# A decoder trunk's attention stage: the second half's query projections in two-tile passes spread over the units, rows turned eight steps behind their tile, norm sums issued later

## The chip, the cores and the metric

The kernel runs on one core of one Trainium2 chip. The metric is the time of one execution on the device in microseconds (us); lower is better. Before the change three runs gave a median of 1218.23 us, from 1217.66 to 1218.72. The engines of a core are TensorE (PE in the profile, with its weight loads as PEld), VectorE (DVE), ScalarE (ACT), GpSimd (POOL) and SyncE (SP). Each runs its own instructions in the order in which they were built and waits on semaphores for the others; DMA queues are fed by SP and POOL.

## The reference

512 tokens of width 1024, batch 1, float32 throughout. A recurrent layer comes first (norm, gated linear recurrence, output projection, feed-forward), then keys and values are made once from its result, then an attention layer (8 query heads of 128 in two groups that share a key/value head, three dilated windows) and a second feed-forward. The change lies in the attention layer, and one line of it in the first norm. Cut to that:

```
h = x + recurrent_mixer(rms_norm(x, a_norm), ...);  h = h + swiglu(rms_norm(h, a_ffn_norm), ...)
k, v = shared_kv(h, ...)                            # per dilation group g = 0, 1, 2: k normed, rotated
q = (rms_norm(h, b_norm) @ b_w_q)                   # 512 x (3 groups x 8 heads x 128)
q = rope(rms_norm(q, b_q_norm[g]))                  # per head
for each group g, window / dilation (128/1, 512/4, 2048/16):
    s = q k^T / sqrt(128), masked to the band;  p = exp(s - max) / sum
    o_g, lse_g = p v, max + log(sum)
o = sum over g of softmax(lse)_g * o_g              # so: one softmax over the keys of all groups
h = h + o @ b_w_o;  h = h + swiglu(rms_norm(h, b_ffn_norm), ...)
```

## The kernel before, in words

**Numbers.** A float32 product is made of three fp32r matmuls. Each operand is split into a rounded high half (xh, wh, qh, kh, ph, vh) and the remainder as a low half (xl, wl, ql, kl, pl, vl), and high·high, low·high and high·low are summed in PSUM (L146 to L148; in the row projections L703 to L705). Splitting an activation is an ACT copy (L228) and a DVE subtraction (L229).

**Weights.** They come as a stream of 128x1024 pieces in order of use (class Stream). SP loads a piece into wr (L85; two buffers), ACT copies it to the high half wh (L100). For the pieces of the attention layer ACT then writes the negated piece to wl (L103), and POOL issues a DMA that reads the piece from memory once more and adds it to wl (L104). Three buffers of wh and wl; in the attention stage a piece is split two pieces ahead of its use.

**Row projections.** `project` takes four pieces, each with two of the eight 128-row blocks of the inner dimension and 512 output columns (four heads). For each piece it goes over the token tiles of 128 given to it; the six matmuls of one piece and tile are a *step*, behind which the generator yields. So a pass over four tiles is 16 steps, one over two tiles is 8 steps, and each reads its four pieces once. When a tile is complete, `collect` has DVE write the gained rows to kn (L637), ACT square them in place (L639) and DVE reduce the squares to sqc (L640). One step later the first 32 elements of each head are rotated (four DVE instructions, L649 to L652). One step after a pass's last tile the normalising factors are made (L661 and the eight small instructions of `rsqrt`, L210 to L219), then a tile's rows are scaled at each step (L669), and `lag` steps after the last tile, one tile a step, PE transposes them (L781) and ACT copies them out as qt (L783). A step is counted by `tick`; `at(steps, fn)` queues work for a later tick.

**Attention.** It runs over 32 units (half kv, query block n, phase p). Unit u's scores are multiplied at stage u (L146 to L148 on kh and qh; the first unit of a block also has the query halves made from qt, L228 and L229), followed by the softmax: masked minimum on DVE (L846 to L849), exponential on ACT (L854), reciprocal on DVE (L855), scaling on POOL (L856). Three units later PE transposes the probabilities pr (L868) and they are split into ph and pl; four units later, at every second unit, the values are multiplied. The first half (kv = 0) has its queries projected ahead of all this; the second half's projections and the first half of the output projection fill PE between the units.

**What sets the order.** The filling is a table written by hand. Each entry names a generator, how many steps of it are given, and over which stretch of units these are spread evenly:

```
drain(itertools.islice(q1, START_Q))          # START_Q = 11 steps ahead of the first unit
plan = [(q1, 40 - START_Q, 0, 12), (q1, 4, 12, 15), (q1, 4, 15, 18.5), (o0, 16, 20, 37)]
```

Here q1 is the second half's projections: groups 0 and 1 over all four tiles, group 2 first over tiles 0 and 1, then over 2 and 3, so its four pieces come twice. o0 is the first half of the output projection. The finished outputs of the first half are split into xh and xl (`move`) when the 4 steps of the second entry have been given, because they take the place of the projections' input. Since a tick is also counted at every second stage of the units, a lag in steps is shorter than that many projections.

The softmax and the split of the turned probabilities are built at high priority, so a scheduler may put them ahead of other work on DVE and ACT. In the first norm, too, the sums are built at high priority.

**The first norm.** The input projection starts on unnormalised rows, and the norm factors are made meanwhile. `in_block(2)` and `in_block(3)` call `between` behind one of their eight inner steps: in block 2 it issues the matmuls of the column sums of squares (L245), in block 3 those that spread the factors over rows.

Of the kernel before, what the change touches and what calls it, by code (L numbers as in the profile page):

```python
# [15 lines left out]
F32 = mybir.dt.float32  # L16
# [123 lines left out]
def trunk(tc, A, out):  # L140
# [11 lines left out]
    def add_pieces(aps, kind="", but=0):  # L152

        start = len(pieces)
        pieces.extend((a, "" if but and i % but == 0 else kind) for i, a in enumerate(aps))
        return start
# [11 lines left out]

    p_f1 = ffn_pieces("f1_in", "f1_out")
    p_kv = add_pieces([A["w_kv"][i] for i in range(12)])  # L170
    p_q = add_pieces([A["w_q"][i] for i in (*range(24), *range(20, 24))], "dma")
    p_o = add_pieces([A["w_o"][i] for i in range(8)], "dma")
    p_f2 = ffn_pieces("f2_in", "f2_out")

    with tc.tile_pool(name="keep", bufs=1) as kp, tc.tile_pool(name="wts", bufs=3) as wp, \
# [104 lines left out]
        with tc.tile_pool(name="lru", bufs=2) as lp, \  # L280
# [16 lines left out]
            def in_block(i, tag="mm", between=None):  # L297
                ps = bank(tag)
                wh, wl = ws.get(i)
                for k in range(KB):  # L300
                    c = slice(128 * k, 128 * k + 128)
                    mm3(ps, (wh[:, c], wl[:, c]), (xh[k], xl[k]), k == 0, k == KB - 1)
                    if k == 2 and between:
                        between()
                return ps

# [188 lines left out]
        with tc.tile_pool(name="tables", bufs=1) as rp:  # L495
# [14 lines left out]
            with tc.tile_pool(name="att", bufs=2) as ap:  # L510
                ap = Pool(ap)
# [12 lines left out]
STATS = 5  # L524
N_PR = 4
LAG_T, LAG_V = 3, 4
START_Q = 11


def rotary(tc, A, rp, tp):  # L530
# [67 lines left out]
def attention(tc, A, ap, ws, env):  # L598
# [30 lines left out]
    def collect(raw, nh, j, n, st, tab, g_row):  # L629

        if j == 0:
            st["sq"] = ap.tile([128, n * nh], F32, name="sqc", tag=f"sqc{nh}").rearrange("q (t i) -> q t i", i=nh)
            st["kn"] = []
        dst = ap.tile([128, 512], F32, name="kn", tag="kn", bufs=N_KN)
        rows = raw[:, :128 * nh]
        x = dst.rearrange("q (h d) -> q h d", d=128)[:, :nh]
        V.tensor_tensor(x, rows.rearrange("q (h d) -> q h d", d=128),  # L637
                        grow[:, g_row].unsqueeze(1).to_broadcast([128, nh, 128]), ALU.mult)
        S.activation(rows, rows, AF.Square)  # L639
        V.tensor_reduce(st["sq"][:, j], rows.rearrange("q (i d) -> q i d", i=nh), mybir.AxisListType.X, ALU.add)  # L640
        st["kn"].append(dst)
        at(1, lambda: rotate(x, nh, tab))
# [48 lines left out]
    def project(p0, xh, xl, done, tiles=range(4)):  # L691

        ps = [None] * 4
        for kk in range(4):
            wh, wl = ws.get(p0 + kk)
            for t in tiles:
                r = slice(128 * t, 128 * t + 128)
                if kk == 0:
                    ps[t] = bank(next(free))
                for k2 in range(2):  # L700
                    k = 2 * kk + k2
                    c = slice(512 * k2, 512 * k2 + 512)
                    PE.matmul(ps[t], xh[k][:, r], wh[:, c], start=k == 0, stop=False)  # L703
                    PE.matmul(ps[t], xh[k][:, r], wl[:, c], start=False, stop=False)  # L704
                    PE.matmul(ps[t], xl[k][:, r], wh[:, c], start=False, stop=k == 7)  # L705
                if kk == 3:
                    done(t, ps[t])
                tick()
                yield
# [59 lines left out]
    qt = {}  # L769

    def project_q(kv):
        for g in range(3):

            for j, tiles in enumerate((range(2), range(2, 4)) if kv and g == 2 else (range(4),)):
                def done_q(t, ps, g=g, st={}, tiles=tiles):
                    collect(ps, 4, t - tiles[0], len(tiles), st, t, 3 + g)
                    if t == tiles[-1]:
                        def turn(j, rows):
                            pt = bank("PT")
                            for i in range(4):  # L780
                                PE.transpose(pt[:, 128 * i:128 * i + 128], rows[:, 128 * i:128 * i + 128], ident)  # L781
                            q = ap.tile([128, 4, 4, 32], F32, name="qt", bufs=12)
                            S.copy(q, pt.rearrange("q (h p i) -> q p h i", h=4, p=4))  # L783
                            qt[j, kv, g] = q
                            if not kv and not j:
                                query_part(0, 0, g)

                        normed(st, 4, 0, turn, 8 if len(tiles) > 2 else 5, tiles)

                yield from project(p_q + 12 * kv + 4 * g + 4 * j, xh, xl, done_q, tiles)  # L790

    def first(fn):

# [9 lines left out]
    def query_part(kv, n, g):  # L803
        if kv and n % 2:
            tags = (f"kh{g}0", f"kl{g}0", 1)
        else:
            tags = ("qh", "ql", 3)
        qh, ql = [ap.tile([128, 512], F32R, name=x, tag=x, bufs=tags[2]) for x in tags[:2]]
        halve(qt.pop((n, kv, g)).rearrange("q p h i -> q (p h i)"), qh, ql)
        qs_[kv, n, g] = qh, ql  # L810
# [127 lines left out]
    drain(project_q(0))  # L938
    q1, o0 = project_q(1), out_half(0, lambda m: None)
    drain(itertools.islice(q1, START_Q))  # L940
    plan = [(q1, 40 - START_Q, 0, 12), (q1, 4, 12, 15), (q1, 4, 15, 18.5), (o0, 16, 20, 37)]
    given, stage = [0] * len(plan), {}
    for k, u in enumerate(attend()):
        stage[u] = stage.get(u, 0) + 1
# [92 lines left out]
```

## Time and profile before

| | |
|---|---|
| median of three runs | 1218.23 us (1217.66 to 1218.72) |
| the profiled execution's own time | 1220.25 us |
| its span | 1218.3 us |
| mean granted clock of PE | 0.998 |
| busy, share of the span: PE | 1204.8 us, 99% |
| DVE | 658.2 us, 54% |
| ACT | 514.4 us, 42% |
| POOL | 157.2 us, 13% |
| weight pieces of w_q, each loaded once and added once by DMA | 28 x 512 KB |

The profile is one execution taken by the hardware profiler. Its span runs from the first instruction to the last. Busy times of engines overlap and don't add up to the span. In a timeline row stand the start, the duration, the engine, the line of the kernel, the operation with its output and inputs, and in brackets the idle time in front of it on its engine and what ended that. In a group's row stand the number of instructions, their busy time with the mean of one in ns, and the idle time in front. Matmuls are pipelined, so that consecutive rows of PE overlap and the time of a block is best taken from the start of one row to the start of another. The attention stage with its projections lies at about 640 to 830 us of the span; its units fill about 690 to 825 us.

### The profile page before, as it was taken

How to read it: one execution, taken by the hardware profiler on the slowest of the kernel's cores; microseconds unless marked ns; L12 is line 12 of the kernel's file. 1: busy time of each engine (PE TensorE's matmuls, PEld its weight loads, DVE VectorE, ACT ScalarE, POOL GpSimd, SP SyncE). 2: the span in 40 equal slices, each digit the busy share in tenths (PEclk: the TensorE clock that was granted, in tenths of full speed). 3: DMA queues.
4: the chain of work that ended last, by engine and by line, in shares of the span. 5: the costliest groups of instructions: out<-in, count | busy, mean ns of one | idle time of the engine just before them, and what ended most of it. 6: DMA issues, size and time to landing. Idle time of an engine off the chain costs nothing.

```text
span 1218.3 us, 14685 instructions
## 1 busy us (share of the span) xinstructions
PE 1204.8 (99%) x5627; PEld 995.6 (82%) x5627; DVE 658.2 (54%) x1237; ACT 514.4 (42%) x758; POOL 157.2 (13%) x159
## 2 busy tenths in 40 slices
PE   8999999999999999999999999999999999999998
PEld 6778888888888888888888887898888888888887
DVE  7787674454544333377564567765554455542221
ACT  6795433233232222265555667655423232222110
POOL 0100001011110000010411243341011011110000
PEclk9999999999999999999999999999999999999999
DMA  6643333323233333333988666335223323233341
GB/s 237 145 104 104 104 106 104 104 87 103 87 103 100 89 100 96 100 96 94 227 179 178 135 153 151 79 70 137 88 87 104 103 88 104 87 100 112 113 115 44
DMA packets 40757, 137.62 MB, mean 113 GB/s; under 512 B 5104, under 2 KB 5744, under 8 KB 40688
## 3 DMA queue, kind: packets, MB, share of 16 engines
q1 hardware_dynamic: 32976, 112.00, 28.9%
q0 software_dynamic: 6704, 23.60, 11.0%
q10 hardware_dynamic: 1008, 1.09, 0.3%
q8 instruction: 44, 0.72, 0.2%
q14 instruction: 25, 0.20, 0.0%
HBM read 133.53 MB, written 2.10 MB: 111 GB/s over the span
## 4 chain that ended last, share of the span: by engine, by line
PE 94%; DVE 3%; ACT 2%; DMA 1%; issue 0%; SPq 0%; DVEq 0%; ACTq 0%
PE ps L147 25%; PE ps L148 25%; PE ps L146 25%; PE ps L703 5%; PE ps L705 5%; PE ps L704 5%; DMA wr<-in_w_in 1%; PE ps L781 1%; PE ps L868 1%; PE ps L387 1%; PE ps L386 1%; ACT wh L100 0%; DVE sqc L640 0%; PE ps L245 0%; DVE pl L229 0%
## 5 line engine op out<-in xcount | busy, mean ns | idle before, releaser
L100 ACT CAST wh<-wr 128x1024 fp32r<-128x1024 f32 (+3 forms) x212 | 215.4, 1017 | 480.9 <-PE ps L147 444.3
L146 PE MATMUL ps<-xh,wh 128*128 128x512 f32 x896 | 352.7, 394 | 0.6 <-ACT xh L223 0.6
L148 PE MATMUL ps<-xh,wl 128*128 128x512 f32 x896 | 349.5, 390 | 0.4 <-DVE wl L107 0.4
L147 PE MATMUL ps<-xl,wh 128*128 128x512 f32 x896 | 349.4, 390 | 0.1
L107 DVE TENSOR_TENSOR wl<-wr,wh 128x1024 fp32r<-128x1024 f32 (+2 forms) x169 | 240.9, 1426 | 148.3 <-ACT wh L100 148.2
L146 PEld LDWEIGHTS ps<-xh,wh 128*128 128x128 f32 x896 | 168.3, 188 | 37.5 <-ACT xh L223 1.5
L147 PEld LDWEIGHTS ps<-xl,wh 128*128 128x128 f32 x896 | 168.5, 188 | 36.1 <-issue 1.7
L148 PEld LDWEIGHTS ps<-xh,wl 128*128 128x128 f32 x896 | 168.4, 188 | 35.8 <-DVE wl L107 0.8
L146 PE MATMUL ps<-gh,wh 128*128 128x512 f32 x352 | 137.0, 389 | 0.0
L148 PE MATMUL ps<-gh,wl 128*128 128x512 f32 x352 | 136.9, 389 | 0.0
L147 PE MATMUL ps<-gl,wh 128*128 128x512 f32 x352 | 136.9, 389 | 0.0
L491 POOL TENSOR_TENSOR u<-u,g 128x512 f32<-128x512 f32 x44 | 58.8, 1336 | 503.4 <-ACT wh L100 354.2
L490 DVE TENSOR_TENSOR u<-ps,rb 128x512 f32<-128x512 f32 x44 | 30.4, 691 | 135.9 <-PE ps L148 135.9
L703 PE MATMUL ps<-wh,xh 128*128 128x512 f32 x224 | 91.5, 408 | 0.4 <-DVE sqc L640 0.4
L705 PE MATMUL ps<-wh,xl 128*128 128x512 f32 x224 | 88.0, 393 | 0.0
L704 PE MATMUL ps<-wl,xh 128*128 128x512 f32 x224 | 87.5, 391 | 0.0
L148 PEld LDWEIGHTS ps<-gh,wl 128*128 128x128 f32 x352 | 66.1, 188 | 13.8
L147 PEld LDWEIGHTS ps<-gl,wh 128*128 128x128 f32 x352 | 66.1, 188 | 13.8
L146 PEld LDWEIGHTS ps<-gh,wh 128*128 128x128 f32 x352 | 66.1, 188 | 13.5
L488 DVE TENSOR_TENSOR g<-ps,rb 128x512 f32<-128x512 f32 x44 | 30.4, 691 | 63.7 <-PE ps L148 63.6
L103 ACT ACTIVATE wl<-wr 128x1024 fp32r<-128x1024 f32 x43 | 45.5, 1058 | 21.7 <-PE ps L704 20.8
L856 POOL TENSOR_SCALAR pr<-pr,den 128x512 f32<-128x512 f32 (+2 forms) x32 | 44.8, 1406 | 63.5 <-DVE den L855 60.5
(213 smaller groups left out, 1439.8 us busy)
## 6 DMA issues: line engine op xcount, KB each, us to landing
wr<-in_f_in SPq DMA_DIRECT2D x88, 512.0 KB, 3.5
wr<-in_f_out SPq DMA_DIRECT2D x32, 512.0 KB, 3.5
wr<-in_w_q SPq DMA_DIRECT2D x28, 512.0 KB, 6.5
wl<-in_w_q POOLq DMA_DIRECT2D x28, 512.0 KB, 7.3
wr<-in_w_in SPq DMA_DIRECT2D x14, 512.0 KB, 3.7
wr<-in_f_out SPq DMA_DIRECT2D x16, 384.0 KB, 3.2
wr<-in_w_kv SPq DMA_DIRECT2D x12, 512.0 KB, 3.5
wr<-in_a_out SPq DMA_DIRECT2D x8, 512.0 KB, 3.5
```

Source lines behind the costliest of these rows:

```text
L100: nc.scalar.copy(hi[:, c], r[:, c])
L103: nc.scalar.mul(lo[:, c], r[:, c], -1.0)
L107: a = eng.tensor_tensor(lo[:, c], r[:, c], hi[:, c].bitcast(F32), ALU.subtract)
L146: PE.matmul(ps, wh, xh, start=first, stop=False)
L147: PE.matmul(ps, wh, xl, start=False, stop=False)
L148: PE.matmul(ps, wl, xh, start=False, stop=last)
L488: V.tensor_tensor(g, pair[0], rb, ALU.mult)
L491: G.tensor_tensor(u, u, g, ALU.mult)
L703: PE.matmul(ps[t], xh[k][:, r], wh[:, c], start=k == 0, stop=False)
L704: PE.matmul(ps[t], xh[k][:, r], wl[:, c], start=False, stop=False)
L705: PE.matmul(ps[t], xl[k][:, r], wh[:, c], start=False, stop=k == 7)
L856: G.tensor_scalar(pr[:, :width], pr[:, :width], den, None, ALU.mult)
```

## The change

1. The second half's projections run in five passes: group 0 over four tiles, group 1 over tiles 0 and 1, group 2 over tiles 0 and 1, group 1 over tiles 2 and 3, group 2 over tiles 2 and 3. Group 1's four pieces are therefore read twice as well: 32 pieces of w_q in all, where there were 28. The number of steps, 48, stays.
2. The transposes of a pass begin 8 ticks behind its last tile, for the two passes over tiles 2 and 3 7 ticks. Before, it was 8 for passes over four tiles and 5 for passes over two.
3. The table: 10 steps ahead of the first unit (11 before); 22 over units 0 to 12.5, 12 over 12.5 to 17, 4 over 17 to 18.5 (before 29 over 0 to 12, 4 over 12 to 15, 4 over 15 to 18.5). The output projection's steps end at unit 36 instead of 37. `move` still hangs on the table's second entry, which now ends at unit 17.
4. In the first norm `between` is called behind the sixth inner step of a block instead of behind the third.

```diff
--- before.py
+++ after.py
@@ -168,7 +168,7 @@
 
     p_f1 = ffn_pieces("f1_in", "f1_out")
     p_kv = add_pieces([A["w_kv"][i] for i in range(12)])
-    p_q = add_pieces([A["w_q"][i] for i in (*range(24), *range(20, 24))], "dma")
+    p_q = add_pieces([A["w_q"][i] for i in (*range(24), *range(16, 24))], "dma")
     p_o = add_pieces([A["w_o"][i] for i in range(8)], "dma")
     p_f2 = ffn_pieces("f2_in", "f2_out")
 
@@ -300,7 +300,7 @@
                 for k in range(KB):
                     c = slice(128 * k, 128 * k + 128)
                     mm3(ps, (wh[:, c], wl[:, c]), (xh[k], xl[k]), k == 0, k == KB - 1)
-                    if k == 2 and between:
+                    if k == 5 and between:
                         between()
                 return ps
 
@@ -524,7 +524,7 @@
 STATS = 5
 N_PR = 4
 LAG_T, LAG_V = 3, 4
-START_Q = 11
+START_Q = 10
 
 
 def rotary(tc, A, rp, tp):
@@ -769,25 +769,26 @@
     qt = {}
 
     def project_q(kv):
-        for g in range(3):
-
-            for j, tiles in enumerate((range(2), range(2, 4)) if kv and g == 2 else (range(4),)):
-                def done_q(t, ps, g=g, st={}, tiles=tiles):
-                    collect(ps, 4, t - tiles[0], len(tiles), st, t, 3 + g)
-                    if t == tiles[-1]:
-                        def turn(j, rows):
-                            pt = bank("PT")
-                            for i in range(4):
-                                PE.transpose(pt[:, 128 * i:128 * i + 128], rows[:, 128 * i:128 * i + 128], ident)
-                            q = ap.tile([128, 4, 4, 32], F32, name="qt", bufs=12)
-                            S.copy(q, pt.rearrange("q (h p i) -> q p h i", h=4, p=4))
-                            qt[j, kv, g] = q
-                            if not kv and not j:
-                                query_part(0, 0, g)
-
-                        normed(st, 4, 0, turn, 8 if len(tiles) > 2 else 5, tiles)
-
-                yield from project(p_q + 12 * kv + 4 * g + 4 * j, xh, xl, done_q, tiles)
+
+        early, late, every = range(2), range(2, 4), range(4)
+        passes = [(0, every), (1, early), (2, early), (1, late), (2, late)] if kv else [(g, every) for g in range(3)]
+        for j, (g, tiles) in enumerate(passes):
+            def done_q(t, ps, g=g, st={}, tiles=tiles):
+                collect(ps, 4, t - tiles[0], len(tiles), st, t, 3 + g)
+                if t == tiles[-1]:
+                    def turn(j, rows):
+                        pt = bank("PT")
+                        for i in range(4):
+                            PE.transpose(pt[:, 128 * i:128 * i + 128], rows[:, 128 * i:128 * i + 128], ident)
+                        q = ap.tile([128, 4, 4, 32], F32, name="qt", bufs=12)
+                        S.copy(q, pt.rearrange("q (h p i) -> q p h i", h=4, p=4))
+                        qt[j, kv, g] = q
+                        if not kv and not j:
+                            query_part(0, 0, g)
+
+                    normed(st, 4, 0, turn, 7 if tiles is late else 8, tiles)
+
+            yield from project(p_q + 12 * kv + 4 * j, xh, xl, done_q, tiles)
 
     def first(fn):
 
@@ -938,7 +939,7 @@
     drain(project_q(0))
     q1, o0 = project_q(1), out_half(0, lambda m: None)
     drain(itertools.islice(q1, START_Q))
-    plan = [(q1, 40 - START_Q, 0, 12), (q1, 4, 12, 15), (q1, 4, 15, 18.5), (o0, 16, 20, 37)]
+    plan = [(q1, 32 - START_Q, 0, 12.5), (q1, 12, 12.5, 17), (q1, 4, 17, 18.5), (o0, 16, 20, 36)]
     given, stage = [0] * len(plan), {}
     for k, u in enumerate(attend()):
         stage[u] = stage.get(u, 0) + 1
```

One line is added ahead of the attention code, so a line number behind L773 is one higher in the changed kernel (L781 becomes L782).

In the built orders the engines' instructions stand as follows. The first place is PE in the third block of the input projection, where L245 makes the norm sums; before:

```order
L146 MATMUL ps<-xh_74,wh_168 128x512
L147 MATMUL ps<-xl_82,wh_168 128x512
L148 MATMUL ps<-xh_74,wl_169 128x512
L146 MATMUL ps<-xh_75,wh_168 128x512
L245 MATMUL ps<-ones,ssum 128x1 x4
L147 MATMUL ps<-xl_83,wh_168 128x512
L148 MATMUL ps<-xh_75,wl_169 128x512
```

In the changed kernel these rows are the same, word for word, at the same place. No engine's order differs ahead of the attention stage but in line numbers.

The second place is ACT near the end of the projections, about unit 16, where `move` splits the finished outputs (xh_72 and following, L228), the turned probabilities are split (ph, L228) and a last tile of the projections is squared (L639). Before:

```order
L103 ACTIVATE wl_6516<-wr_6513 128x1024
L100 CAST wh_6515<-wr_6513 128x1024
L639 ACTIVATE ps<-ps 128x512
L854 ACTIVATE pr,den<-pr,mn 128x256
L228 CAST xh_72<-ps 128x128
L228 CAST ph<-ps 128x2x128
L228 CAST xh_73<-ps 128x128
L228 CAST qh<-qt 128x512 x2
L228 CAST ph<-ps 128x2x128
```

And now:

```order
L639 ACTIVATE ps<-ps 128x512
L103 ACTIVATE wl_6556<-wr_6553 128x1024
L100 CAST wh_6555<-wr_6553 128x1024
L855 ACTIVATE pr,den<-pr,mn 128x256
L639 ACTIVATE ps<-ps 128x512
L228 CAST xh_72<-ps 128x128
L228 CAST ph<-ps 128x2x128
L228 CAST xh_73<-ps 128x128
L228 CAST qh<-qt 128x512 x2
L228 CAST ph<-ps 128x2x128
```

The exponential, in front of which stand the same two weight operations, now stands ahead of the square of the last tile instead of behind it, and another tile's square stands ahead of the weight operations.

The third place is DVE at the same point of the program. There stand the reduce of that tile (L640), the factors (L661, then L210 to L219 on qr4y and qr4a), and the low halves xl of the outputs and pl of the probabilities (L229), each of which goes with the high half of the same number on ACT. Before:

```order
L640 TENSOR_REDUCE sqc<-ps 128x4
L855 RECIPROCAL den<-den 128x1
L652 TENSOR_TENSOR kn<-ra,rbt 128x4x32
L661 SCALAR_TENSOR_TENSOR sqc<-sqc,epsv 128x8
L210 TENSOR_SCALAR qr4y<-sqc 128x8
L213 TENSOR_TENSOR qr4a<-qr4y,sqc 128x8
L214 SCALAR_TENSOR_TENSOR qr4a<-qr4a,qr4y 128x8
L215 SCALAR_TENSOR_TENSOR qr4y<-qr4a,qr4y 128x8
L216 SCALAR_TENSOR_TENSOR qr4a<-qr4y,sqc 128x8
L217 TENSOR_TENSOR qr4a<-qr4a,qr4y 128x8
L218 SCALAR_TENSOR_TENSOR qr4a<-qr4a 128x8
L229 TENSOR_TENSOR xl_80<-ps,xh_72 128x128
```

And now:

```order
L856 RECIPROCAL den<-den 128x1
L640 TENSOR_REDUCE sqc<-ps 128x4
L661 SCALAR_TENSOR_TENSOR sqc<-sqc,epsv 128x8
L210 TENSOR_SCALAR qr4y<-sqc 128x8
L229 TENSOR_TENSOR xl_80<-ps,xh_72 128x128
L213 TENSOR_TENSOR qr4a<-qr4y,sqc 128x8
L229 TENSOR_TENSOR pl<-ps,ph 128x2x128
L214 SCALAR_TENSOR_TENSOR qr4a<-qr4a,qr4y 128x8
```

The first low half xl_80 stood behind eight steps of the factors and now stands behind two of them; pl follows one step later.

## The prediction

> **What bounds the kernel now.** I read the page first: totals of the engines, then the shares of the chain that ended last.
>
> ```profile
> span 1218.3 us, 14685 instructions
> PE 1204.8 (99%) x5627; PEld 995.6 (82%) x5627; DVE 658.2 (54%) x1237; ACT 514.4 (42%) x758; POOL 157.2 (13%) x159
> PE 94%; DVE 3%; ACT 2%; DMA 1%; issue 0%; SPq 0%; DVEq 0%; ACTq 0%
> ```
>
> TensorE (PE) carries 94% of the chain, and the change neither adds nor removes a matmul. So only the time in which PE waits can be won, and only by waits that the change touches. I therefore went through PE's timeline over the attention stage for rows with idle time in front, in brackets with the releaser. Between 680 and 780 us these are all of them.
>
> ```profile
> 685.74 0.50 PE L703 MATMUL ps<-wh,xh 128*128 128x512 f32 x1 [0.37 <-DVE sqc L640]
> ...
> 734.71 0.66 PE L781 MATMUL ps<-ident,kn 128*128 128x128 f32 x4 [0.69 <-ACT qt L783]
> 738.23 0.35 PE L146 MATMUL ps<-kh,qh 128*128 128x256 f32 x1 [0.47 <-DVE mn L849]
> 745.97 0.63 PE L781 MATMUL ps<-ident,kn 128*128 128x128 f32 x4 [0.80 <-DVE kn L669]
> 758.25 0.33 PE L146 MATMUL ps<-kh,qh 128*128 128x128 f32 x1 [0.64 <-ACT qh L228]
> 768.71 0.30 PE L146 MATMUL ps<-kh,qh 128*128 128x128 f32 x1 [1.02 <-DVE mn L849]
> 776.25 0.38 PE L146 MATMUL ps<-ph,vh 128*128 128x256 f32 x1 [1.69 <-ACT ph L228]
> ```
>
> Their sum is 0.37 + 3.62 (the five from 734.71 to 768.71) + 1.69 = 5.68 us. The windows by stage (per row: window, length, busy time of PE, PEld, DVE, ACT, POOL, granted clock, DMA share, GB/s) add a second loss.
>
> ```profile
> 680.00:780.00 100.00, 94.21 (x589) 82.08 (x588) 72.27 (x251) 69.29 (x130) 36.96 (x32) 0.98 0.65 146
> 720.00:730.00 10.00, 10.00 (x66) 8.91 (x65) 8.46 (x32) 7.04 (x13) 5.36 (x5) 1.00 0.92 215
> ...
> 776.00:778.00 2.00, 1.75 (x6) 1.46 (x7) 2.00 (x11) 1.05 (x5) 0.01 (x1) 0.74 0.39 141
> 778.00:780.00 2.00, 2.00 (x10) 1.90 (x10) 1.70 (x5) 0.78 (x3) 2.00 (x2) 0.50 0.00 0
> 780.00:782.00 2.00, 1.91 (x15) 1.55 (x15) 0.00 (x0) 1.01 (x2) 0.81 (x1) 0.91 0.00 0
> ```
>
> Behind the longest wait the granted clock falls to half: 2 x (0.26 + 0.50 + 0.09) = 1.70 us lost. All that these waits cost is thus 5.68 + 1.70 = 7.4 us, 0.6% of the span. The Trainium skill, page "TensorE: Matmul & The Clock Gate", section "What's actually happening", says that an idle window of about 3.4 us halves the clock, and that the window runs freely; 1.70 us lost at half speed is 3.4 us, so the trace agrees with the length, though PE was not idle for all of it.
>
> **Norm sums issued later: 0.** Their matmuls (L245) stand at the same place in PE's built order in both kernels, and no engine's order differs before the attention stage. So the wait in front of them stays.
>
> ```profile
> 20.22 0.39 PE L146 MATMUL ps<-xh,wh 128*128 128x512 f32 x1
> 21.51 1.02 PE L245 MATMUL ps<-ones,ssum 128*128 128x1 f32 x8 [0.90 <-DVE ssum L237]
> ```
>
> Had the step moved behind this wait, it would be worth up to those 0.90 us; nothing excludes it but the order.
>
> **More weight pieces.** Groups 1 and 2 of the second half now run in two-tile passes, so group 1's four pieces are fetched and split a second time. The prices are in ACT's groups and the DMA queues over 685 to 780 us, and in the times to landing of the low parts (wl) in 720 to 750 us.
>
> ```profile
> L103 ACT ACTIVATE wl<-wr 128x1024 fp32r<-128x1024 f32 x12 | 12.7, 1058 | 3.5 <-PE ps L704 2.7 <-DMA wr<-in_w_q 0.8
> L100 ACT CAST wh<-wr 128x1024 fp32r<-128x1024 f32 x12 | 12.4, 1038 | 0.0
> ...
> q0 software_dynamic: 1872, 6.82, 42.0%
> q1 hardware_dynamic: 1872, 6.82, 22.6%
> ...
> DMA to landing us min/median/max: 7.3/7.4/9.1
> ```
>
> ACT: 4 x (1.058 + 1.038) = 8.4 us more; on its 69.3 busy us of 100 that makes 78. DMA: a piece of 0.524 MB takes 0.420 x 95 x 0.524/6.82 = 3.1 us of the 16 engines for its low part and 0.226 x 95 x 0.524/6.82 = 1.65 us for its load, together 4.7; four make 19 us, and the share of 0.65 becomes 0.84. None of this is on PE; it is hidden as long as a piece lands before PE asks for it. PE's own demand I price by blocks from its timeline:
>
> ```profile
> 750.67 0.33 PE L146 MATMUL ps<-ph,vh 128*128 128x256 f32 x1
> ...
> 752.73 0.44 PE L703 MATMUL ps<-wh,xh 128*128 128x512 f32 x1
> ...
> 754.16 0.60 PE L868 MATMUL ps<-ident,pr 128*128 128x128 f32 x4
> 754.52 0.36 PE L146 MATMUL ps<-kh,qh 128*128 128x256 f32 x1
> ...
> 755.58 0.44 PE L703 MATMUL ps<-wh,xh 128*128 128x512 f32 x1
> ...
> 757.01 0.60 PE L868 MATMUL ps<-ident,pr 128*128 128x128 f32 x4
> ```
>
> A step of six projection matmuls takes 757.01 - 755.58 = 1.43 us, a unit's scores 1.06, a block of transposes at most 0.36, a widest value block 2.06. In the changed order the 16 two-tile pieces hold 32 steps (45.8), 15 score blocks (15.9), 24 transposes (some 8) and seven value blocks of 1.0 to 2.06 (10.7): 80 us, or 5.0 per piece against 4.7 on the DMA engines. The low part of piece i takes the buffer of piece i-3, so from there to its use lie two pieces, 10 us, against ACT's 1.06, POOL's issue and the 7.4 us to landing: it fits, with little to spare. The Trainium skill, page "DMA: Bandwidth & Descriptors", section "Anatomy of one DMA — SWDGE (gpsimd) path", has a fit that gives 3.2 us for 0.524 MB; by it the pieces would be far from the limit and the slow rival below would fall away. It is for one DMA by itself, and the measured 7.4 us decides.
>
> POOL issues the four extra low parts (L104) among the softmax scalings (L856), which PE transposes only three units later; SP's four extra loads have only loads behind them. The first unit one step earlier, and the output projection spread over one unit less, move work within stretches in which PE waits less than 0.4 us: 0.
>
> **The waits inside the passes.** Fewer steps lie between the units now (22 over the first 12.5 units, 29 over 12 before), more in units 12.5 to 18.5 (16 against 8). DVE's prices for what PE waits on are these:
>
> ```profile
> L229 DVE TENSOR_TENSOR ql<-qt,qh 128x512 fp32r<-128x512 f32 x14 | 9.3, 684 | 0.0
> L669 DVE TENSOR_TENSOR kn<-kn,qr4y 128x512 f32<-128x512 f32 x12 | 7.8, 682 | 0.1
> L640 DVE TENSOR_REDUCE sqc<-ps 128x4 f32<-128x512 f32 x10 | 6.8, 685 | 0.2
> ...
> 772.65 0.16 DVE L661 SCALAR_TENSOR_TENSOR sqc<-sqc,epsv 128x8 f32<-128x8 f32 x1
> ...
> 774.51 0.16 DVE L219 SCALAR_TENSOR_TENSOR qr4y<-qr4a,qr4y 128x8 f32<-128x8 f32 x1
> ```
>
> From L661 to L219, the first and last of nine small steps, a pass's factors take 2.0 us. I followed the changed orders of PE, ACT and DVE by hand with these prices. Three waits come out. (a) Group 0's four tiles each give DVE a product, a rotation and a reduce, some 2.2 us, while PE makes a tile in 1.43; with the softmaxes between, DVE is an estimated 4 us behind after the last. Then this tile's own 2.2, the factors (2.0), the first scaled row (0.68) and two softmaxes (some 0.7 each) put that row 10.3 us after the last projection. PE arrives after four steps, two score blocks, a value block and transposes: 9.3. That is 1.0 of waiting, and behind PE's waiting transpose stand the next step and unit 6's scores. (b) At units 8 and 12 the scores stand among the query halves (0.68 each on DVE, after ACT's casts): 0.4 and 0.5. (c) At unit 16 two more such halves, with the next tiles' factors in between: 1.15, where 0.64 stands today. Together 3.05, against 0.37 + 3.62 that go, as the rows they wait for have another place now: -0.94. Bounds: (a) to (c) all covered, -4.0; each doubled, +2.1. I take the worked value, as its rows are this stage's own.
>
> **The last wait** (776.25). The orders of ACT and DVE at this place stand with the change. On ACT the exponential has moved ahead of the last tile's square, so the square comes 0.7 us later. On DVE the seven small steps of the factors (L213 to L219) stood ahead of the half xl that lets ACT go on; in the changed order only two small ones (L661, L210) do.
>
> ```profile
> 771.17 0.58 ACT L639 ACTIVATE ps<-ps 128x512 f32<-128x512 f32 x1
> 771.69 0.49 ACT L854 ACTIVATE pr<-pr,mn 128x256 f32<-128x256 f32 x1
> ...
> 774.63 0.27 ACT L228 CAST xh<-ps 128x128 fp32r<-128x128 f32 x1 [1.74 <-DVE xl L229]
> 774.79 1.14 ACT L228 CAST qh<-qt 128x512 fp32r<-128x512 f32 x2
> 775.83 0.37 ACT L228 CAST ph<-ps 128x256 fp32r<-128x256 f32 x1
> ...
> 771.78 0.69 DVE L640 TENSOR_REDUCE sqc<-ps 128x4 f32<-128x512 f32 x1
> ...
> 774.31 0.28 DVE L229 TENSOR_TENSOR xl<-ps,xh 128x128 fp32r<-128x128 f32 x1
> ```
>
> From reduce to half it is 2.53 us; with two small steps, 0.69 + 0.45, about 1.3 earlier. But the square is 0.7 later, and the weight split ahead of it can start only when piece 135's last low part is used, with another square in front, some 0.7 later again. So the chain ends within 0.3 of where it does today: 1.45 to 2.0, I take 1.45. Then PE meets the low half pl, 0.7 later, with no output projection between, as there is today: 2.15 against 1.69, +0.46. The half clock stays, 1.70 on both sides.
>
> **The sum**: 0 - 0.94 + 0.46 = -0.5 us. The profiled execution took 1220.25 us, its span of 1218.3 and 2.0 around it; the median of the unprofiled runs is 1218.23, so I set the sum against that: 1217.7 us.
>
> **The rivals.**
> 1. The spreading works: DVE and ACT get two tiles at a time, no backlog forms, (a) to (c) are hidden: -4.0, and with a part of the last wait 1213.8 us. For it speaks that five waits sit where four tiles' rows were bunched and steps were few; against it, that units 0 to 12 have less cover now.
> 2. Slower: the weights. Three of the 16 pieces come out of my hand count with no slack (the second two-tile piece, and the two around unit 15, where steps follow closely). A landing of 9.1 instead of 7.4 us, the largest above, makes each 1.7 late: 5.1, less what other waits hide, net +3.5: 1221.7 us. It decides from the point where two pieces of PE work take less than ACT's wait, the issue and the landing. For it: 0.92 DMA share in 720 to 730 us, when two-tile pieces ran before. Against it: PE waited for no transfer there.
> 3. The last wait is broken in two, and the clock stays whole: -1.70 more, 1216.0 us. For it: the 1.02 us at 768.71 left the clock whole; against it, nothing says where the 2.15 would break. By the Trainium skill's free-running window (page and section named above) it is a matter of phase.
>
> **How the numbers follow.** About 0.2% (2.4 us) is what this measurement can tell from no change. Forecast 0.38, rival 1 0.32, rival 2 0.22, rival 3 0.08, which lies on the border and counts half as faster, half as no change. Faster 0.32 + 0.04 = 0.36, same 0.38 + 0.04 = 0.42, slower 0.22. The forecast's own range is 1215.6 to 1219.8 (half of each term's way to its bounds: the norm sums' 0.90, the -4.0 and +2.1, the last wait's 2.0); with the rivals 1213.0 to 1221.6.
>
> **What would show it.** Right: PE's row before L245 keeps about 0.9; the waits between 690 and 775 add to 2 to 4 us, on DVE kn, ql and ACT qh; the last wait is 1.4 to 2.2 with the clock at half behind it. Rival 1: these waits under 1 us. Rival 2: PE's projection rows (L703, L704) wait for DMA wl, or ACT's L103 for DMA wr. Wrong altogether: a wait over 3 us anywhere, or a changed time outside the attention stage.

## The result: slower

The changed kernel took 1223.96 us (four runs, 1223.02 to 1224.37), the kernel before 1218.02 us beside it. The ratio is 1.0047, with a 95% interval from 1.0032 to 1.0062: slower by 5.7 us. The forecast was 1217.7, with a range of 1213.0 to 1221.6 and a chance of 0.22 for slower. The time lies outside the range and on the other side of the forecast.

Head and chain of the changed kernel's page:

```profile
span 1222.6 us, 14721 instructions
PE 1207.9 (99%) x5627; PEld 996.9 (82%) x5627; DVE 659.8 (54%) x1246; ACT 521.6 (43%) x766; POOL 161.0 (13%) x163
PE 86%; ACT 5%; DVE 5%; DMA 2%; issue 1%; ACTq 0%; DVEq 0%
```

PE's matmuls are as many as before. PE's share of the chain fell from 94% to 86%, so PE waited more. The rows of the changed kernel's PE timeline with 0.25 us or more of idle time in front, from 680 to 850 us:

```profile
692.41 0.66 PE L782 MATMUL ps<-ident,kn 128*128 128x128 f32 x4 [0.39 <-DVE kn L669]
723.81 0.35 PE L146 MATMUL ps<-kh,qh 128*128 128x256 f32 x1 [0.28 <-DVE mn L850]
737.42 0.50 PE L704 MATMUL ps<-wl,xh 128*128 128x512 f32 x1 [0.71 <-DMA wl<-in_w_q]
753.36 0.30 PE L148 MATMUL ps<-kh,ql 128*128 128x64 f32 x1 [0.95 <-DVE ql L229]
774.42 0.58 PE L146 MATMUL ps<-ph,vh 128*128 128x256 f32 x1 [1.94 <-ACT ph L228]
792.13 0.38 PE L146 MATMUL ps<-ph,vh 128*128 128x256 f32 x1 [0.55 <-ACT ph L228]
792.80 0.39 PE L147 MATMUL ps<-pl,vh 128*128 128x256 f32 x1 [0.29 <-DVE pl L229]
808.23 0.38 PE L146 MATMUL ps<-ph,vh 128*128 128x256 f32 x1 [1.04 <-ACT ph L228]
816.81 0.39 PE L147 MATMUL ps<-vl,vh 128*128 128x256 f32 x1 [0.34 <-DVE vl L229]
825.67 0.39 PE L146 MATMUL ps<-ph,vh 128*128 128x256 f32 x1 [1.58 <-ACT ph L228]
```

The first five stand where the projections fill PE, and there they are five where before had seven. The last five are the news. They sum to 3.80 us and stand in the part in which the output projection fills PE, where before had 0.29. All stand in front of a value block, which needs both halves of the turned probabilities (named ph and pl, or vh and vl in the row at 816.81, where they lie in other buffers).

Where the two profiles part is seen at rows that both have. L245 makes the norm sums, at the start of the program and once more behind the attention stage. First before, then the change:

```profile
789.31 0.55 PE L868 MATMUL ps<-ident,pr 128*128 128x128 f32 x3
858.72 0.95 PE L245 MATMUL ps<-ones,ssum 128*128 128x1 f32 x8
```

```profile
20.03 1.02 PE L245 MATMUL ps<-ones,ssum 128*128 128x1 f32 x8
788.64 0.48 PE L146 MATMUL ps<-xh,wh 128*128 128x512 f32 x1
863.20 0.95 PE L245 MATMUL ps<-ones,ssum 128*128 128x1 f32 x8
```

The rows at 789.31 and 788.64 have the same number in PE's order, behind the last of the turned queries. Up to there the change is 0.67 us ahead. From there to the second L245 the same work takes 858.72 - 789.31 = 69.4 us before and 863.20 - 788.64 = 74.6 us in the change, 5.1 us more. To the end of the span the two differ by 0.2 us. So the whole loss lies behind 788 us. Of the 5.1, 3.80 - 0.29 = 3.5 is idle time that the profile names; the remaining 1.6 lies, by the distances between the starts of rows, mostly in value and score blocks, whose first matmuls follow each other more slowly.

The lead of 0.67 comes from 21.51 - 20.03 = 1.5 us at the very start, where the 0.90 us ahead of the first L245 are gone, less 0.8 us that the program gave back afterwards. Run e3 below tells whether the start belongs to the change.

Why the value blocks wait is seen from one place in both kernels. In the kernel before, PE and then ACT:

```profile
803.09 0.62 PE L868 MATMUL ps<-ident,pr 128*128 128x128 f32 x4
...
804.52 0.45 PE L146 MATMUL ps<-xh,wh 128*128 128x512 f32 x1
...
805.94 0.28 PE L146 MATMUL ps<-ph,vh 128*128 128x256 f32 x1
```

```profile
803.75 0.59 ACT L228 CAST ph<-ps 128x512 fp32r<-128x512 f32 x1 [0.21 <-PE ps L868]
804.82 0.72 ACT L854 ACTIVATE pr<-pr,mn 128x512 f32<-128x512 f32 x1 [0.49 <-DVE mn L849]
...
807.94 1.03 ACT L100 CAST wh<-wr 128x1024 fp32r<-128x1024 f32 x1
```

In the changed kernel, PE and then ACT:

```profile
805.61 0.60 PE L869 MATMUL ps<-ident,pr 128*128 128x128 f32 x4
805.97 0.36 PE L146 MATMUL ps<-kh,kh 128*128 128x256 f32 x1
```

```profile
805.94 0.73 ACT L855 ACTIVATE pr<-pr,mn 128x512 f32<-128x512 f32 x1 [1.72 <-DVE mn L850]
...
806.66 1.03 ACT L100 CAST wh<-wr 128x1024 fp32r<-128x1024 f32 x1
807.60 0.57 ACT L228 CAST ph<-ps 128x512 fp32r<-128x512 f32 x1
```

In the changed kernel the probabilities are turned at 805.61 and PE has only one score block (about 1.1 us) before the value block needs them. On ACT the exponential and a weight cast of 1.03 us stand ahead of the cast of ph, which begins at 807.60. In the kernel before the transposes begin at 803.09, and a step of the output projection (804.52 to 805.94) stands between the score block and the value block and covers the wait. The order on ACT has moved as well: before, ph is cast at 803.75, ahead of the exponential (804.82), and the weight cast comes later (807.94). The PE timelines show the same difference at five of the six value blocks behind 788 us; ahead of the sixth the change has a step again. With T for a block of transposes, S for scores, O for a step of the output projection and V for a value block, two units read:

```
before   at first  O T S T O S V     later  T O S T S O V
change             O T S O T S V
```

The number of steps between two value blocks is the same, two. In the kernel before, one of them always stands between the second T and the V; in the change both stand ahead of it. Of these five value blocks of the change, the three that wait for ph (792.13, 808.23, 825.67) are those for which a weight cast (L100) stands right in front of the cast of ph on ACT. The two without it (799.59, 816.09) don't wait for ph. So two things act together, less cover on PE and a later ph on ACT, and no run here separates them.

### The profile page after: what moved, and what is told of

It reads as the page before. It is cut to its first block, busy times and chain, and to the rows that moved or that the text cites. A ratio compares the mean times of both kernels' runs of the same rounds, so it can differ in the third digit from the quotient of the medians.

```text
span 1222.6 us, 14721 instructions
## 1 busy us (share of the span) xinstructions
PE 1207.9 (99%) x5627; PEld 996.9 (82%) x5627; DVE 659.8 (54%) x1246; ACT 521.6 (43%) x766; POOL 161.0 (13%) x163
## 4 chain that ended last, share of the span: by engine, by line
PE 86%; ACT 5%; DVE 5%; DMA 2%; issue 1%; ACTq 0%; DVEq 0%
PE ps L147 24%; PE ps L148 23%; PE ps L146 23%; PE ps L704 5%; PE ps L703 5%; PE ps L705 5%; ACT wh L100 1%; DVE xc L380 1%; PE ps L782 1%; DMA wl<-in_w_q 1%; ACT wl L103 1%; DMA wl<-in_w_in 1%; DMA wr<-in_w_o 1%; DVE ql L229 0%; ACT ph L228 0%
## 5 line engine op out<-in xcount | busy, mean ns | idle before, releaser
L100 ACT CAST wh<-wr 128x1024 fp32r<-128x1024 f32 (+3 forms) x216 | 219.4, 1017 | 479.8 <-PE ps L147 439.9
L147 PEld LDWEIGHTS ps<-xl,wh 128*128 128x128 f32 x896 | 168.6, 188 | 36.5 <-issue 1.7
L103 ACT ACTIVATE wl<-wr 128x1024 fp32r<-128x1024 f32 x47 | 49.8, 1060 | 24.8 <-PE ps L704 21.8
L228 ACT CAST gh<-u 128x512 fp32r<-128x512 f32 x44 | 27.4, 622 | 60.7 <-POOL u L491 60.7
```

What stands on the lines that cost most here:

```text
L100: nc.scalar.copy(hi[:, c], r[:, c])
L103: nc.scalar.mul(lo[:, c], r[:, c], -1.0)
L147: PE.matmul(ps, wh, xl, start=False, stop=False)
```

## Experiments

The runs were made in three rounds on three chips, where the kernel before had medians of 1219.17 (e1 to e4), 1219.48 (e5 to e8) and 1219.12 us (e9 to e11). What is compared are the ratios to before, with their 95% intervals.

### Is it the spread of the output projection? Take it out of the change, put it alone into before

```diff
 e1: the changed kernel with
-    ..., (o0, 16, 20, 36)]
+    ..., (o0, 16, 20, 37)]
 e2: the kernel before with
-    ..., (o0, 16, 20, 37)]
+    ..., (o0, 16, 20, 36)]
```

> The changed kernel with the output projection's steps spread to unit 37 again, as before; passes, lags, start and norm step stay changed. Theory (the shorter spread is the loss): between the transposes that follow the last query turn and the end of the stage, the change took 4.97 us longer for the same work (44.4 against 39.4 us), because each value block now follows the transposes it depends on by one score block only; with 37 this goes: 1224.0 - 5.0 = 1219.0. Rival (the four extra weight pieces or the later turns are the loss): it stays at 1224.0. Half and half: 1221.5.

> The kernel before with only the output projection's end moved from unit 37 to 36. Theory (the shorter spread is the loss): 1218.0 + 5.0 = 1223.0, with waits of PE on the high halves ph ahead of the value blocks at four places. Rival (it needs the rest of the change): 1218.0.

With unit 37 the changed kernel took 1218.9 against 1219.17: ratio 1.000, 0.9989 to 1.0010. The kernel before with unit 36 took 1224.36: ratio 1.0043, 1.0027 to 1.0058, or 5.2 us. This one number makes the change slow, and alone it makes the kernel before slow. The traces say the same: from the matmul at 789.31 in before (the same number in PE's order everywhere) to the second L245, before takes 69.4 us, the change 74.6, e1 69.3 and e2 74.1. In the second kernel the waits have come to the same places:

```profile
792.41 0.39 PE L147 MATMUL ps<-pl,vh 128*128 128x256 f32 x1 [0.20 <-DVE pl L229]
807.86 0.38 PE L146 MATMUL ps<-ph,vh 128*128 128x256 f32 x1 [1.04 <-ACT ph L228]
816.44 0.39 PE L147 MATMUL ps<-vl,vh 128*128 128x256 f32 x1 [0.34 <-DVE vl L229]
825.31 0.39 PE L146 MATMUL ps<-ph,vh 128*128 128x256 f32 x1 [1.56 <-ACT ph L228]
```

### The pace, or the place within the unit?

```diff
 e9: the changed kernel with
-    ..., (o0, 16, 20, 36)]
+    ..., (o0, 16, 20.5, 36.5)]
```

> The changed kernel with the output projection's steps over units 20.5 to 36.5 instead of 20 to 36: the same pace of one step per unit, half a unit later. Theory (not the pace is the loss but the step's place in the unit: it must stand between the second block's transposes and the value block that needs them): the steps then stand there, as with 20 to 37, and the time is that of the first run: before - 0.3. Rival (the pace: 16 steps over 16 units leave too little at the end): it stays near before + 5.

It took 1218.58 against 1219.12: ratio 0.9991, 0.9982 to 1.0001. The pace is that of the slow kernel, the time that of the fast one. What costs the 5 us is that the steps come due at the first stage of each unit and so stand ahead of the transposes; half a unit later they stand behind the last scores (T O S T S O V), ph is cast ahead of the exponential again (802.66 and 803.60), and the stretch from 789.31 on takes 69.1 us.

### The norm step alone

```diff
 e3: the kernel before with
-                    if k == 2 and between:
+                    if k == 5 and between:
```

> The kernel before with only the norm sums' call moved from the third to the sixth inner step. No instruction changes its place on any engine. Theory (the wait ahead of the norm sums was shorter in the changed kernel's profile because a weight piece happened to land sooner in that execution): 1218.0, and the wait lies anywhere from 0 to 0.9. Rival (the edit removes the 0.90 and 0.39 us of waiting): 1216.7.

1218.78 against 1219.17: ratio 0.9999, 0.9991 to 1.0008. No gain of 1.3 us. In its profile the norm sums did not wait:

```profile
20.12 1.02 PE L245 MATMUL ps<-ones,ssum 128*128 128x1 f32 x8
```

But they did not wait in the profile of e5 below either, which has the old step, and they did in that of e7, which has the new one. First e5, then e7:

```profile
19.93 1.02 PE L245 MATMUL ps<-ones,ssum 128*128 128x1 f32 x8
```

```profile
20.61 1.02 PE L245 MATMUL ps<-ones,ssum 128*128 128x1 f32 x8 [0.72 <-DVE ssum L237]
```

What differs between the profiles of before and of the change, whose ACT rows follow, is when a weight piece lands on which ACT waits:

```profile
16.14 1.05 ACT L100 CAST wh<-wr 128x1024 fp32r<-128x1024 f32 x1 [1.47 <-DMA wr<-in_w_in]
```

```profile
14.22 1.05 ACT L100 CAST wh<-wr 128x1024 fp32r<-128x1024 f32 x1
```

So the wait at the start lies anywhere from 0 to 0.9 us in these profiles, with either step, and the 1.5 us that the changed kernel's profile had gained there isn't the change's. That a late landing is behind it every time isn't shown: in e9 PE waited 0.35 us there, and ACT did not wait for that piece.

### The lags

```diff
 e4: the changed kernel with (o0, 16, 20, 37) and
-                    normed(st, 4, 0, turn, 7 if tiles is late else 8, tiles)
+                    normed(st, 4, 0, turn, 8 if tiles is every else 5, tiles)
 e5: the kernel before with
-                        normed(st, 4, 0, turn, 8 if len(tiles) > 2 else 5, tiles)
+                        normed(st, 4, 0, turn, 7 if kv and tiles[0] else 8, tiles)
```

> As the first of these runs (changed kernel, output projection to unit 37), but the rows of the two-tile passes are turned 5 steps behind their tile as before, instead of 8 and 7. Theory (the longer lag covers DVE's chain of reduce, factors and scaling): waits on kn come back, about 0.5 us at each of the four two-tile passes, 1219.0 + 2.0 = 1221.0. Rival (a longer lag only moves the wait to the query halves): 1219.0 or less.

> The kernel before with only the lags changed: the two two-tile passes are turned 8 and 7 steps behind their last tile instead of 5. Theory (the lag is worth something by itself, since the same lags in the changed kernel were worth 1.9 us against 5): of the waits of before that lie behind the two-tile passes, 0.64 at 758 and 1.02 at 768 us, about 1 us goes: before - 1.0. Rival (lag and passes only work together, since the waits of before at 735 to 746 us come from four-tile passes): before +- 0.3.

With the old lags the changed passes took 1220.82 against 1219.17: ratio 1.0013, 1.0004 to 1.0022, about 1.9 us more than e1. On kn, waits came back (PE timeline of e4):

```profile
715.45 0.66 PE L782 MATMUL ps<-ident,kn 128*128 128x128 f32 x4 [0.80 <-DVE kn L669]
738.67 0.63 PE L782 MATMUL ps<-ident,kn 128*128 128x128 f32 x4 [0.35 <-DVE kn L669]
761.21 0.66 PE L782 MATMUL ps<-ident,kn 128*128 128x128 f32 x4 [0.48 <-DVE kn L669]
```

They sum to 1.63 us at three of the two-tile passes; the theory had 0.5 at each of four. But in the two profiles other waits went in exchange: one for mn is 1.24 us in e1 and 0.29 in e4, and the waits for weight pieces (0.37 and 0.43 in e1) are gone. From matmul 2750, ahead of the stage, to the second L245 e1 takes 229.1 us and e4 229.2. In the profiles the wait has thus only moved, as the rival had it. e4's profiled execution, the slowest of its eleven, lost its time ahead of the changed code, where a weight piece came late and a window at half clock followed (609.69 to 613.10):

```profile
608.91 0.50 PE L704 MATMUL ps<-wl,xh 128*128 128x512 f32 x1 [1.92 <-DMA wl<-in_w_q]
```

Where the other executions of e4 lose the 1.9 us stays open. The new lags in the old passes gave 1218.49 against 1219.48: ratio 0.9994, 0.9986 to 1.0003. That is -0.7 us with 0 inside the interval, and it doesn't decide between -1.0 and no effect. The waits that were to go, at 758 and 768 us, were still there in its profile with 0.68 and 0.92. So by the times alone the changed passes with the old lags cost some 1.6 us, and the new lags give about that back; together they are worth nothing that can be measured (e1).

### The last wait and the half clock behind it

In all kernels so far PE waits 1.7 to 2.7 us for ph at about 775 us, and in the profiles of all but e5 the granted clock falls to half around its end. A step of independent work in front of this value block was tried in both kernels.

```diff
 e6, e7, e10: the changed kernel, with the lag 4 for group 2's pass over tiles 2 and 3, and
-    ..., (q1, 4, 17, 18.5), (o0, 16, 20, 36)]
+    ..., (q1, 4, 17, 20.5), (o0, 16, 20, 37)]       # e6
+    ..., (q1, 4, 18, 20.5), (o0, 16, 20, 37)]       # e7
+    ..., (q1, 4, 17, 20.5), (o0, 16, 20.5, 36.5)]   # e10
 e8, e11: the kernel before, with the lag 4 for the last pass, and
-    ..., (q1, 4, 15, 18.5), ...
+    ..., (q1, 4, 18, 20.5), ...                     # e8
+    ..., (q1, 4, 15, 20.5), ...                     # e11
```

> As the first run (changed kernel, output projection to unit 37), but the last four projection steps are spread over units 17 to 20.5 instead of 17 to 18.5, and group 2's last pass is turned 4 steps behind its tile instead of 7, so that a projection step stands between the second block's transposes and the value block that waited 2.31 us there. Theory (this wait and the half clock behind it are one loss, which a step of 1.43 us of independent work shrinks): the wait falls to about 0.9 and the clock stays whole, 1.4 + 1.7 = 3 us less than the first run. Rival (ACT and DVE are what is late there, and the step brings its own square and reduce): the wait only moves, 0 to 0.5 us less.

> As the run before, but the last four steps over units 18 to 20.5, so that one step stands ahead of and one behind the last score block in front of that value block (2.9 us of independent work). Theory: the wait goes wholly, with the half clock: 2.3 + 1.7 = 4 us less than the first run. Rival: as above, with a new wait of 1 us or more on the last turned rows or query halves: no more than 1 us less.

> The kernel before with only its last four projection steps over units 18 to 20.5 instead of 15 to 18.5, turned 4 steps behind their tile instead of 5. Theory (the last wait and its half clock are worth 1.69 + 1.70 in any of these kernels): before - 3.4, less what the units 15 to 18 lose in cover (up to 1). Rival: new waits at units 15 to 18 take it all: before.

> The kernel of the run with the late steps over units 17 to 20.5 (before - 4.1), with the output projection over units 20.5 to 36.5 instead of 20 to 37. Theory: the same place within the unit, the same time, before - 4.1 (+- 0.5). Rival (a pace that stays even to the end takes the 0.29 us on pl at 820 us as well): before - 4.6.

> The kernel before with its last four projection steps over units 15 to 20.5 instead of 15 to 18.5, turned 4 steps behind their tile. In the run with units 18 to 20.5 three short waits (0.57, 0.52, 0.67) at 756 to 764 us were followed by 17 us at half clock while PE was never idle, in a stretch of value and score blocks with small matmuls and no projection step. Theory (there the stretch without wide matmuls held the clock down, and a step in it prevents that): no half clock behind 764, and without the wait at 776: before - 3. Rival (moving these steps in the old passes costs cover at units 15 to 18 however it is done): before + 0 or slower.

| run | against before | ratio, interval |
|---|---|---|
| e6, change, 17 to 20.5 | 1215.65, 1219.48 | 0.9966, 0.9954 to 0.9979 |
| e7, change, 18 to 20.5 | 1215.42, 1219.48 | 0.9968, 0.9956 to 0.9979 |
| e10, as e6, output projection 20.5 to 36.5 | 1215.09, 1219.12 | 0.9968, 0.9958 to 0.9978 |
| e8, before, 18 to 20.5 | 1225.11, 1219.48 | 1.0043, 1.0030 to 1.0057 |
| e11, before, 15 to 20.5 | 1218.00, 1219.12 | 1.0004, 0.9990 to 1.0018 |

In the changed kernel it worked. e6 is 4.1 us faster than before and, by the ratios, as much faster than e1; its theory had 3. The wait at 775 is gone; what took its place is a wait of 0.73 for turned rows, and the clock stayed whole:

```profile
753.48 0.30 PE L148 MATMUL ps<-kh,ql 128*128 128x64 f32 x1 [0.80 <-DVE ql L229]
...
779.94 0.66 PE L782 MATMUL ps<-ident,kn 128*128 128x128 f32 x4 [0.73 <-DVE kn L669]
```

A second step in front (e7) and the even pace (e10) gave nothing more that can be told apart; e10's interval holds its theory's -4.1 and its rival's -4.6. The rivals' numbers for e6 and e7 (no more than 1 us less than e1) are out. These three beat both kernels. The later steps and the lag of 4 were only run together.

In the kernel before, both expectations for e8 fell: 5.2 us slower. Its waits are small. But the windows of PE (length, busy time, granted clock, DMA share, GB/s) show this:

```profile
757.57:760.99 3.42, 2.90 (x19) 1.00 0.78 196
760.99:764.40 3.41, 2.74 (x23) 1.00 0.58 113
764.40:781.47 17.07, 17.07 (x71) 0.50 0.25 50
781.47:784.88 3.41, 3.41 (x22) 1.00 0.23 64
```

For 17.07 us PE was never idle and ran at half clock, 8.5 us lost. Without them e8 would be at about -3.3, near the theory's -3.4; that is worked out and was not run. All five executions of e8 had a mean clock of 0.993 to 0.995. e11 was to prevent this with a projection step, because its expectation took e8's stretch for one without such steps. That reading was wrong; two steps stand in it, among them these matmuls:

```profile
773.36 0.63 PE L703 MATMUL ps<-wh,xh 128*128 128x512 f32 x1
...
778.27 0.63 PE L703 MATMUL ps<-wh,xh 128*128 128x512 f32 x1
```

In e11 another one falls at 762.66 us. The edit kept the clock whole in only part of its executions: eight of twelve had a mean clock of 0.998 or more and took 1216.5 to 1219.2 us, four had 0.993 or 0.994 and took 1221.6 to 1224.2. Its profiled execution is one of the four, with 13.66 us at half clock:

```profile
759.79:763.20 3.41, 2.91 (x21) 1.00 0.72 138
763.20:776.86 13.66, 13.66 (x57) 0.50 0.37 84
```

## Why the prediction was wrong, step by step

**The step that failed** is the sentence that put the first unit's earlier start and the output projection's spread at 0, because they "move work within stretches in which PE waits less than 0.4 us". For the output projection it was worth +5.2 us (e2), and +5.1 by the profiles. That PE waits little in a stretch shows that the work there is in a good order, not that its order doesn't matter: the steps of the output projection were the cover of the value blocks, and one unit of seventeen less moved a step to the other side of the transposes at five of the six value blocks behind 788 us, and put a weight cast ahead of ph on ACT at three of them. The rule was in the prediction itself: it priced the last wait at 2.15 because no step of the output projection stood between the use of ph and that of pl any more. It was applied at this one block and not at those behind it, whose order could have been read in the same way. With the term at +5.1 the sum would have been 1218.2 - 0.5 + 5.1 = 1222.8, 1.2 us below the measured time, which is what the interval of e1 leaves open.

**The other terms.** With the output projection back at unit 37 the prediction's -0.5 stood against a measured ratio of 1.000 (-1.3 to +1.2 us), so the rest of the sum holds, though not each part of it:

- Norm sums, 0: right (e3). That the wait "stays" was not: in the profiles it is 0 to 0.9 us with either step.
- Waits inside the passes, 3.05 foreseen: in the changed kernel 0.39 + 0.28 + 0.71 + 0.95 = 2.3, and 2.9 and 2.7 in the profiles of e1 and e9, which are the same program up to there. (a) was 0.39 instead of 1.0. (b) was nothing at unit 8 instead of 0.4, and 0.28 at unit 12 (723.81) instead of 0.5. (c), at unit 16 (753.36), was 0.95 instead of 1.15. The 0.71 for a weight piece was not in the sum.
- The last wait, 2.15 with 1.70 for the clock: 1.94 in the changed kernel, 2.31 in e1 and 2.67 in e9. In the changed kernel's profile the clock was at half for two windows instead of one, and PE was still idle at the start of the first:

```profile
770.25:773.66 3.41, 2.23 (x21) 1.00 0.89 161
773.66:777.08 3.42, 2.66 (x10) 0.50 0.84 220
777.08:780.49 3.41, 3.41 (x13) 0.50 0.00 0
780.49:783.90 3.41, 3.31 (x24) 1.00 0.00 0
```

- The forecast's own range: by its rule, half of each term's way, it comes to 1215.7 to 1219.5 and not 1215.6 to 1219.8. Nothing hangs on that.

**The rivals.** Rival 1 didn't come: by the times, the new passes with the old lags are slower than before (e4), and with the new lags the same (e1). Rival 2 had the right side and the wrong cause. Its sign, a projection row that waits for wl, is there, with 0.71 us and not 3.5. Rival 3, the whole clock, didn't come in the changed kernel's profile, but its mechanism is what e6, e7 and e10 use: with the wait broken up the clock stays whole in their profiles. Of what was to show the prediction wrong, "a changed time outside the attention stage" did not occur but for the start, which differs between executions, and no wait was over 3 us. What did occur, five waits of 0.3 to 1.6 ahead of value blocks behind 790 us, was not on the list.

## What to carry to other kernels

Where filling work stands between dependent blocks of an engine that runs in order, its amount per round says little: look at which side of the producing instruction each piece falls on, for every consumer, and write the order of one round down before and after. Do so for each engine in the chain: here one move on PE also changed what stands ahead of ph on ACT. A stretch without waits is not a stretch with slack. And a table of due times that is moved by a few per cent can shift every piece by one place when the new rate hits the boundaries of the stages exactly (one step per unit), which a half-unit offset undoes.

## What the hardware did that was not expected

**The half clock comes in whole windows, and where their borders fall differs between executions.** Where a trace here shows half clock inside the program, the stretch lasts 3.41, 6.83, 13.65 or 17.07 us, which are 1, 2, 4 and 5 times 3.413. The clock first becomes whole anywhere from 4.20 to 10.05 us after the span's start. The same kernel may have some or none: of eleven executions of e9, two had a mean clock of 1.000 and took 1214.3 and 1214.8 us, and seven had 0.997 and took 1218.9 on average, 4 us more. The clock isn't all of it: the one execution of e5 at 1.000 took 1218.05 us, in the midst of those at 0.998 and 0.999. In e5 the wait of 1.67 us fell across the border of two windows, and no half clock followed:

```profile
771.36:774.78 3.42, 2.59 (x24) 1.00 0.98 189
774.78:778.19 3.41, 2.57 (x15) 1.00 0.36 118
778.19:781.60 3.41, 3.41 (x25) 1.00 0.00 0
```

That is what the Trainium skill says of it (page "TensorE: Matmul & The Clock Gate", section "What's actually happening"): a window of 3413 ns that runs freely, so that the point of change depends on where in it the work falls. These traces agree with the length and the free phase.

**Busy is not enough to get the clock back.** The window ahead of e8's half clock had PE busy for 2.74 of 3.41 us, more than the 2.57 and 2.59 above that did no harm, and then the clock came back only behind the fifth window, though PE had no idle time in any of them. The section of the Trainium skill's page named above has the clock return after at least one busy window of about 3.4 us; by PE's busy time as the profile shows it, four such windows in e8 and three in e11 passed without that. A lack of 512-column steps doesn't explain it, since both stretches hold some.

What separates the windows better is an estimate from the thirteen traces: the number of columns of the matmuls that begin in a window. Of the some 4500 windows at whole clock (up to 1195 us), ten were followed by half clock. Nine of these ten had fewer than 3200 columns, and of the others only five had. By busy time the ten reach up to 2.91 us, and 58 of the others had no more. That fits narrow matmuls counting for less, but it is a count and no experiment. For the way back it separates less well: 2304 to 4096 columns in the last window of a half-clock stretch, 2048 to 3072 in the windows before it. What is counted stays open.
